# Every fifth piece of the mixer's weights: its low part on GpSimd instead of VectorE

## The chip, the core and the metric

One core of one Trainium2 chip runs the whole program. The metric is device time in microseconds for one execution; each version is run several times and the median counts.

## What is computed

A decoder trunk of two layers over 256 tokens of width 1024, in float32. Cut to what matters here:

```python
for layer in range(2):
    y   = h @ w_in[layer]                  # 256x1024 @ 1024x3672: q, k, v, gates, indexer of three mixers
    mix = concat(gla(y), moba(y), dsa(y)) @ w_out[layer]      # w_out 1024x1024
    h   = layer_norm(alpha * h + mix)
    h   = layer_norm(alpha * h + moe(h))   # router, 16 experts of width 512, top 2
```

`w_in` and `w_out` are the mixer's weights; the experts' weights are not touched by the change.

## The kernel before

**Stages.** The profiled span shows two layers. The mixer of layer 0 runs from 0 to about 146 us, its experts to about 355, the mixer of layer 1 from 355 to about 501, its experts to the end. Weights stream in over SyncE's queue into 33 feed buffers (`wf`) and are used once.

**The split product.** In the mixer, a matrix product in float32 is made of three products in the faster type fp32r. Activations and weights are each split into a high part (rounded to fp32r) and a low part (what the rounding lost), and TensorE adds high x high, high x low and low x high in one PSUM bank. In the trace the weights' parts are `whi` and `wlo`, the activations' `hhi` and `hlo`. ScalarE makes `whi` by a copy with rounding; VectorE makes `wlo` by subtracting `whi` from the weights `wf`, so that this subtraction has two inputs in SBUF.

**Pieces.** The class `Pieces` (line 573) does this for the weights. `weight_pieces(l)` writes the plan of a layer in the order in which TensorE wants it: groups I (16 pieces of 292 columns), V (8 of 512), GV (16 of 264), M, S, GK, GG (8 of 512 each) from `w_in`, then 16 of 512 from `w_out`; 88 in all, counted from 0 by `self.i`. Before TensorE takes piece j, `fill` makes the pieces up to j + `ahead` (4 in most of the mixer, 5 in the first group, 3 for `w_out`). When all pieces of a feed buffer are made, `more()` issues the next weight DMA. In layer 1 the first two pieces are made ahead of the layer norm by `fill(pool)` (line 1648), so their low parts are GpSimd's already. The first group of each layer multiplies the first 128 tokens in plain float32 with unsplit weights, then the other 128 with the pieces.

**What else is on the engines.** VectorE has, among other things, the indexer's sums (`acc`, a chain of eight dependent operations for each score block, then loops of max and replace), the rotary embedding (`rope`, on `yk` and `yq`), softmax steps, and the split of the activations of layer 1 (`hlo`). GpSimd has the powers of the norms, a memset for the linear attention (`aM`), and in layer 1 two operations on the 128x1024 tile `z`, a multiply and an add (`pool.tensor_mul(z, z, g2)`, `pool.tensor_add(z, z, b2)`), both called a z multiply below for short.

**The order.** The schedule is written by hand (`manual_schedule`): each engine runs its list strictly in the order in which the program emits it. The class `Order` keeps an estimated clock for each engine; generators wait ("yield") until something they need is due by these clocks, and so the estimates decide which operation is emitted next. `_Lane.cost` has the estimates: 1.04 n + 65 ns for a subtraction of n columns on VectorE, 2.2 n + 50 on GpSimd (lines 205 to 215). All operations go through one helper, so that the profile puts nearly all on its line 235; operations are told apart by their tiles.

Of the kernel before, what the change touches and what calls it, by code (L numbers as in the profile page):

```python
# [9 lines left out]
F32 = mybir.dt.float32  # L10
# [34 lines left out]
N_T4 = 9  # L45
N_SM = 10
N_WS = 4
N_WO = 3
N_UNITS = ((1, 3), (2, 6))
N_WARM0 = 7  # L50
# [189 lines left out]
def trunk_kernel(ctx, tc, x, positions, w_in, gate_up, gate_bias, norm_gain, w_out, ln_mix_g, ln_mix_b,  # L240
# [8 lines left out]
    pe, act, dve, pool = od.pe, od.act, od.dve, od.pool  # L249
# [9 lines left out]
    def t2(name, shape=(P, 512), dt=F32):  # L259
        return wp.tile(list(shape), dt, name=name, tag="t2", bufs=N_T2)  # L260
# [80 lines left out]
    def more(n=1):  # L341
        for _ in range(n):
            while issued[0] < len(specs) and specs[issued[0]][0] in extra:
                issued[0] += 1
            if issued[0] >= len(specs):
                return
            key, (parts, nk, w) = specs[issued[0]]
            issued[0] += 1
            t = fp.tile([P, nk, w], F32, name="wf", tag="wf")
            for at, src in parts:  # L350
                nc.sync.dma_start(t[:, at[0], at[1]] if at else t.rearrange("p k n -> p (k n)"), src)
            feed[key] = t
# [220 lines left out]
    class Pieces:  # L573
# [8 lines left out]
        def fill(self, eng=dve):  # L582
            while self.i < len(self.plan) and self.i < self.j + self.ahead:
                key, kk, c0, n = self.plan[self.i]
                src = feed[key][:, kk, c0:c0 + n]
                hi = t2("whi", (P, n), F32R)
                lo = t2("wlo", (P, n), F32R)
                act.activation(hi, src, AF.Copy)
                eng.tensor_sub(lo, src, hi.bitcast(F32))
                units[key] = feed[key]  # L590
                self.made[self.i] = hi, lo
                self.left[key] -= 1
                if not self.left[key]:
                    feed.pop(key)
                    more()
                self.i += 1
# [72 lines left out]
    def weight_pieces(l):  # L669
# [5 lines left out]
        for k0 in OUT_ORDER:  # L675
            plan += [((l, "O", k0 + kk), 0, 512 * n, 512) for kk in range(2) for n in range(2)]
        return Pieces(plan, N_WS)

# [83 lines left out]
    for l in range(DEPTH):  # L762
        done = set()

        def project(widths, res, first, step):
# [3 lines left out]
            if first:  # L769
                pieces.ahead = N_AHEAD  # L770
                for k in range(KT):
# [9 lines left out]
                    yield None  # L781
                pieces.ahead = N_WS
            for k in range(KT):
# [339 lines left out]
        def backbone():  # L1123
# [28 lines left out]
            n_done = 0  # L1152
            pieces.ahead = N_WO
            for k0 in OUT_ORDER:
# [559 lines left out]
```

## Time and profile before

| | |
|---|---|
| median of 3 runs | 723.16 us (722.4 to 724.0) |
| the profiled execution | 724.48 us |
| its span, first to last instruction | 722.8 us |
| TensorE busy | 696.5 us (96%) |
| VectorE busy | 440.6 us (61%) |
| ScalarE busy | 267.9 us (37%) |
| GpSimd busy | 43.9 us (6%) |
| granted TensorE clock, mean | 0.989 |
| DMA | 244.05 MB, 338 GB/s |

Engines are called PE (TensorE), PEld (its weight load), DVE (VectorE), ACT (ScalarE), POOL (GpSimd). A row of the order of time gives the start in us, the length, engine, line, operation, the tiles (out<-in), the shape, how many were merged into the row, and in brackets the engine's idle time just before, with what ended it. Busy shares are averages over stages that differ; the mixers are 292 us of the span.

### The profile page before, as it was taken

To read this page: it belongs to the slowest core of one execution; us is meant where nothing else is said; L and a number is where in the kernel's file an instruction comes from. 1 tells how busy PE (TensorE), PEld (TensorE's weight loads), DVE (VectorE), ACT (ScalarE), POOL (GpSimd) and SP (SyncE) were. 2 spreads that over 40 slices of the span, in tenths; PEclk is the share of its full clock that TensorE was granted. 3 is DMA by queue.
4 is the path that set the end of the run, shared out by engine and by line. 5 is a ranking of instruction groups with operands and counts; after the bars stand their busy time and mean duration, and the time that the engine had idled before them with its cause. 6 is when DMAs were issued, how large, how long until landed. Compare 5 with 4: busy or idle time off the path is not lost. (4 is left out here: it accounts for less than half of the span.)

```text
span 722.8 us, 11139 instructions
## 1 busy us (share of the span) xinstructions
PE 696.5 (96%) x3829; PEld 405.7 (56%) x3829; DVE 440.6 (61%) x1115; ACT 267.9 (37%) x547; POOL 43.9 (6%) x72
## 2 busy tenths in 40 slices
PE   9999999999999989999899999999999999999993
PEld 8897977853533533533488889777535334343330
DVE  6787865650635455767488688757243546358645
ACT  5667655431312112212186666464213112022121
POOL 2000001000000001210130000011000000011002
PEclk9999999999999999999999999999999999999997
DMA  9799945869999999999999754469699999999971
GB/s 308 274 388 408 409 162 204 298 225 408 408 404 408 406 406 409 407 409 408 333 391 400 306 184 163 152 227 338 236 409 409 403 407 408 406 409 409 408 301 58
DMA packets 83533, 244.05 MB, mean 338 GB/s; under 512 B 10180, under 2 KB 14344, under 8 KB 83464
## 3 DMA queue, kind: packets, MB, share of 16 engines
q1 hardware_dynamic: 82792, 242.91, 88.1%
q8 instruction: 34, 0.56, 0.3%
q10 hardware_dynamic: 416, 0.26, 0.1%
q14 instruction: 35, 0.29, 0.1%
q0 software_dynamic: 256, 0.03, 0.0%
HBM read 242.13 MB, written 1.05 MB: 336 GB/s over the span
## 5 line engine op out<-in xcount | busy, mean ns | idle before, releaser
L235 PE MATMUL gu<-wf,xT 128*64 128x512 f32 x912 | 226.0, 594 | 3.5 <-PEq L1430 3.5
L235 PEld LDWEIGHTS gu<-wf,xT 128*64 128x64 f32 x912 | 71.8, 137 | 131.7 <-issue 123.6
L235 DVE SCALAR_TENSOR_TENSOR yt<-y,ws,yt 32x512 fp32r<-32x512 f32 (+1 forms) x116 | 86.7, 748 | 94.6 <-ACT yt L235 93.2
L235 DVE TENSOR_TENSOR wlo<-wf,whi 128x512 fp32r<-128x512 f32 (+2 forms) x174 | 97.2, 598 | 44.5 <-ACT whi L235 40.3
L235 PE MATMUL y<-wf,actT 128*64 128x512 f32 x432 | 110.5, 595 | 1.8 <-ACT actT L235 1.8
L235 ACT ACTIVATE whi<-wf 128x512 fp32r<-128x512 f32 (+2 forms) x176 | 86.8, 551 | 16.5 <-PE po L235 9.5
L235 PE MATMUL pj<-whi,hhi 128*128 128x512 f32 (+2 forms) x224 | 81.7, 365 | 0.0
L235 PE MATMUL pj<-wlo,hhi 128*128 128x512 f32 (+2 forms) x224 | 78.1, 349 | 1.7 <-DVE wlo L235 1.5
L235 PE MATMUL pj<-whi,hlo 128*128 128x512 f32 (+2 forms) x224 | 77.7, 347 | 0.0
L235 ACT ACTIVATE yt<-y,ws 128x512 fp32r<-128x512 f32 x60 | 36.9, 687 | 104.2 <-PE y L235 91.1
L235 PEld LDWEIGHTS y<-wf,actT 128*64 128x64 f32 x432 | 34.2, 137 | 53.8 <-issue 40.5
L235 DVE TENSOR_TENSOR act<-act,gu 128x512 f32<-128x512 f32 x16 | 11.0, 688 | 83.9 <-PE gu L235 64.9
L235 PE MATMUL gu<-wx,xT 128*64 128x512 f32 x112 | 52.7, 596 | 0.0
L235 PEld LDWEIGHTS pj<-whi,hhi 128*128 128x128 f32 x224 | 42.1, 188 | 8.2 <-issue 2.9
L235 PEld LDWEIGHTS pj<-wlo,hhi 128*128 128x128 f32 x224 | 42.1, 188 | 7.2 <-DVE wlo L235 3.5
L235 PEld LDWEIGHTS pj<-whi,hlo 128*128 128x128 f32 x224 | 42.0, 188 | 5.2
L235 ACT ACTIVATE actT<-aT 128x512 f32<-128x512 f32 x16 | 9.5, 595 | 85.3 <-PE aT L235 76.7
L235 ACT ACTIVATE xT<-xT,cols 128x256 f32<-128x256 f32 x32 | 17.4, 564 | 60.1 <-PE xT L235 60.1
L235 ACT ACTIVATE act<-gu 128x512 f32<-128x512 f32 x16 | 9.6, 597 | 76.2 <-PE gu L235 76.2
L235 PE MATMUL y<-wx,actT 128*64 128x512 f32 x80 | 33.4, 595 | 0.0
L235 DVE TENSOR_TENSOR z<-z,sc 128x512 f32<-128x512 f32 x48 | 29.7, 680 | 0.4 <-PE sc L235 0.4
L235 DVE TENSOR_SCALAR xT<-xT,cols 128x256 f32<-128x256 f32 x32 | 16.9, 543 | 14.7 <-ACT xT L235 14.3
(269 smaller groups left out, 938.0 us busy)
## 6 DMA issues: line engine op xcount, KB each, us to landing
wf<-in_w_expert_gate_dram SPq DMA_DIRECT2D x114, 512.0 KB, 10.2
wf<-in_w_expert_up_dram SPq DMA_DIRECT2D x114, 512.0 KB, 9.9
wf<-in_w_expert_down_dram SPq DMA_DIRECT2D x108, 512.0 KB, 10.1
wf<-in_w_in_dram SPq DMA_DIRECT2D x32, 512.0 KB, 9.9
wx<-in_w_expert_down_dram SPq DMA_DIRECT2D x36, 256.0 KB, 6.0
wf<-in_w_out_dram SPq DMA_DIRECT2D x16, 512.0 KB, 11.0
wx<-in_w_expert_up_dram SPq DMA_DIRECT2D x24, 256.0 KB, 6.7
wx<-in_w_expert_gate_dram SPq DMA_DIRECT2D x10, 512.0 KB, 7.4
```

The source lines that it names most:

```text
L235: return fn(*a, **kw)
```

## The change

A constant and one expression. In `Pieces.fill`, the subtraction of the pieces with index 4, 9, 14, ... goes to GpSimd's list (`pool`), the others stay with `eng`, which is VectorE except in the call `fill(pool)`. The planner then books the subtraction on GpSimd's clock with GpSimd's estimate.

```diff
+SHARE = 5
@@ class Pieces, fill
                 act.activation(hi, src, AF.Copy)
-                eng.tensor_sub(lo, src, hi.bitcast(F32))
+                (pool if self.i % SHARE == SHARE - 1 else eng).tensor_sub(lo, src, hi.bitcast(F32))
```

## Rows read from the trace of the kernel before

**Rows 1.** Busy time by stretch (engine busy and count, PEclk, DMA share, GB/s).

```profile
0.00:146.00 146.00, 144.18 (x901) 120.00 (x905) 107.11 (x319) 87.97 (x194) 9.43 (x33) 1.00 0.85 307
...
355.00:501.00 146.00, 143.19 (x899) 117.38 (x900) 112.62 (x304) 88.60 (x196) 13.43 (x12) 1.00 0.75 269
```

**Rows 2.** TensorE's waits, 0 to 146 us: total, times, longest.

```profile
PE pj L235 <- DVE wlo L235: 0.7, 1, 0.7
```

**Rows 3.** TensorE's waits, 355 to 501 us.

```profile
PE pj L235 <- DVE wlo L235: 0.8, 2, 0.6
```

**Rows 4.** Groups by form: count, busy us, mean ns, idle before.

```profile
L235 DVE TENSOR_TENSOR wlo<-wf,whi 128x512 fp32r<-128x512 f32 x112 | 73.5, 686 | 36.0 <-ACT whi L235 33.7 <-PE po L235 2.0
...
L235 POOL TENSOR_TENSOR wlo<-wf,whi 128x292 fp32r<-128x292 f32 x2 | 1.6, 806 | 46.3 <-ACT whi L235 46.3
```

**Rows 5.** Order of time: GpSimd's work on z and VectorE beside it.

```profile
365.19 2.51 POOL L235 TENSOR_TENSOR z<-z,vec 128x1024 f32<-128x1024 f32 x1 [3.08 <-PE tr L235]
...
367.00 1.25 DVE L235 TENSOR_TENSOR hlo<-hT,hhi 128x512 fp32r<-128x512 f32 x1 [0.24 <-ACT hhi L235]
...
367.77 2.70 POOL L235 TENSOR_TENSOR z<-z,vec 128x1024 f32<-128x1024 f32 x1
...
368.17 2.86 DVE L235 TENSOR_TENSOR hlo<-hT,hhi 128x512 fp32r<-128x512 f32 x1
...
358.23 0.75 DVE L235 SCALAR_TENSOR_TENSOR z<-z,mv,vec 128x512 f32<-128x512 f32 x1
...
714.65 1.26 POOL L235 TENSOR_TENSOR z<-z,vec 128x512 f32<-128x512 f32 x1 [0.34 <-ACT z L235]
...
714.94 1.53 DVE L235 SCALAR_TENSOR_TENSOR z<-z,mv,vec 128x512 f32<-128x512 f32 x1
```

**Rows 6.** Layer 0 near 60 us: order of time; groups up to 62.2 us.

```profile
57.48 1.29 DVE L235 TENSOR_TENSOR wlo<-wf,whi 128x512 fp32r<-128x512 f32 x2 [3.45 <-ACT whi L235]
...
58.90 0.62 ACT L235 ACTIVATE whi<-wf 128x512 fp32r<-128x512 f32 x1
...
59.66 2.68 DVE L235 SCALAR_TENSOR_TENSOR acc<-rl,wi,acc 128x128 f32<-128x128 f32 x7
62.26 1.89 DVE L235 TENSOR_TENSOR wlo<-wf,whi 128x512 fp32r<-128x512 f32 x3
...
63.00 0.50 PE L235 MATMUL pj<-wlo,hhi 128*128 128x512 f32 x1 [0.73 <-DVE wlo L235]
...
L235 DVE TENSOR_TENSOR wlo<-wf,whi 128x292 fp32r<-128x292 f32 (+2 forms) x47 | 22.0, 519 | 12.9 <-ACT whi L235 12.9
```

**Rows 7.** The same place in layer 1, order of time.

```profile
415.07 0.62 ACT L235 ACTIVATE whi<-wf 128x512 fp32r<-128x512 f32 x1
...
416.06 0.34 DVE L235 SCALAR_TENSOR_TENSOR acc<-rl,wi,mc 128x128 f32<-128x128 f32 x1
...
419.03 0.68 DVE L235 TENSOR_TENSOR wlo<-wf,whi 128x512 fp32r<-128x512 f32 x1
...
419.77 0.50 PE L235 MATMUL pj<-wlo,hhi 128*128 128x512 f32 x1
```

**Rows 8.** The start of layer 1: pieces 4, 9 and those after.

```profile
364.47 0.44 ACT L235 ACTIVATE whi<-wf 128x292 fp32r<-128x292 f32 x1
...
369.78 0.43 ACT L235 ACTIVATE whi<-wf 128x292 fp32r<-128x292 f32 x1
...
372.16 4.18 DVE L235 TENSOR_TENSOR wlo<-wf,whi 128x292 fp32r<-128x292 f32 x11
...
372.66 0.40 PE L235 MATMUL pj<-wlo,hhi 128*128 128x292 f32 x1 [0.57 <-DVE wlo L235]
```

**Rows 9.** Layer 1, piece 19 and the rope chain.

```profile
377.48 0.62 ACT L235 ACTIVATE whi<-wf 128x512 fp32r<-128x512 f32 x1
...
378.48 0.16 DVE L235 TENSOR_TENSOR rope<-yk,rc 128x16 f32<-128x16 f32 x1
...
381.64 0.33 PE L235 MATMUL tr<-ident,yk 128*128 128x128 f32 x1 [0.20 <-DVE yk L235]
```

## The prediction

> **What bounds the kernel now.** I read the table of busy time by stretch first, since the change touches only the two mixers (0 to 146 and 355 to 501 us). In it the reader is to see that TensorE is busy 144.18 of 146 us in the first mixer and 143.19 of 146 in the second, VectorE 107.11 and 112.62, ScalarE 88, GpSimd 9.43 and 13.43, with the granted clock at 1.00, which is the 2.4 GHz level [rows 1]. So TensorE sets the pace, VectorE is three quarters full, and GpSimd is nearly free. The second view is what TensorE waited for in each mixer. In the first only one wait on a low part (wlo) stands, 0.7 us; in the second two, 0.8 us together [rows 2, 3]. All that a lighter VectorE could give back directly is therefore about 1.5 us of some 289. The third view is the order of time around these waits and around GpSimd's work: a kernel whose TensorE is this full gains or loses only where a wlo comes just in time or too late.
>
> **What is moved.** Each layer's plan has 88 pieces (16 of 292 columns, 16 of 264, 56 of 512). Of the indices 0 to 87, those with remainder 4 by five are 4, 9, ... 84: 17 a layer, 34 in all (3 of 292, 4 of 264, 10 of 512 in each layer). The high part stays on ScalarE, no DMA moves, and no piece changes its place on TensorE's list by itself.
>
> **Taken from VectorE.** A 512-column subtraction lasts 0.686 us [rows 4]; back to back they start (1.89 - 0.68) / 2 = 0.60 us apart [rows 6]. 34 pieces at no more than that are under 20.4 us of the 219.7 us that VectorE is busy in both mixers. Off TensorE's path this is worth nothing.
>
> **Added to GpSimd.** It has made two 292-column low parts already: 0.806 us each [rows 4]. For 512 columns the nearest row is its z multiply of 128x512, 1.26 us [rows 5]. Per layer 3 x 0.81 + 4 x about 0.75 + 10 x 1.26 = 18 us (0.75 is an estimate for 264 columns from the two rows), on an engine idle for over 130 of 146. A moved piece is thus about 0.6 us slower than VectorE would be alone, but pieces are made three to five ahead, and a moved one no longer queues behind VectorE's other work. I cost the longer latency at nothing; the cover is the other pieces that TensorE multiplies meanwhile, and if it were gone, a piece would cost up to 0.6 us.
>
> **What the two engines do to each other** is the term that decides. In layer 1 GpSimd multiplies z at 365.19 (2.51 us) and again at 367.77 (2.70 us, to 370.48). VectorE's subtractions hlo <- hT - hhi have the form of wlo (two SBUF inputs, fp32r out, 512 columns). The first, 367.00, takes 1.25 us and ends 0.55 after GpSimd's first; the second, 368.17, takes 2.86 us and ends 371.03, again 0.55 after GpSimd's second [rows 5]. Alone such an operation takes 0.69 [rows 4]. So VectorE stands still until GpSimd is through. The second z multiply in turn waited for the first hlo (to 368.25) and then needed 2.23 us, where the undisturbed one took 2.51: about 0.28 us of GpSimd's time is a start that needs no memory port. The three-operand form does the same: z <- z,mv,vec takes 1.53 us at 714.94 beside GpSimd and 0.75 at 358.23 without it [rows 5]. The price of one moved piece to a busy VectorE is hence 1.26 - 0.28 = 0.98 us for 512 columns (0.81 - 0.28 = 0.53 for 292), against 0.60 (0.37) given back later, where the piece's own turn would have been: VectorE gets slower, not faster, while it has two-input work queued. The bounds of one meeting are 0 (it finds VectorE idle or with a PSUM operand) and 0.98.
>
> The Trainium skill (SBUF — State Buffer, section Who interferes with whom) says that a VectorE instruction with two SBUF inputs and a GpSimd instruction that reads SBUF exclude each other, the second one blocking fully. By that rule the trace agrees (2.86 us), and were the port merely shared, a meeting would cost about half and the sum below 1.7 us. The skill (Perfetto Trace Analysis, section Optimizing Scalar/DVE Operations) allows offloading to GpSimd if VectorE is saturated, and warns that it might not help between these two; here VectorE is not saturated (107 of 146 us).
>
> **Where it lands on TensorE's path.** Pieces are counted by wlo in VectorE's list: 47 of them (0 to 46) start before 62.2 [rows 6].
> 1. Layer 0, piece 49. Its high part ends at 58.90 + 0.62 = 59.52 [rows 6]. GpSimd starts near 59.58 and wants the port at 59.86, inside the chain of eight acc operations (two SBUF inputs each; the last seven from 59.66, 2.68 us). It gets it at the next joint, 60.02, and holds it to 61.0, so the third operation (60.05) is 0.95 late. Behind the chain stand the wlo of pieces 47, 48 and 49 at 62.26; TensorE already waits for 47 (63.00, idle 0.73) [rows 6]. So +0.95. That piece 49 is no longer third there helps nobody: TensorE is at 47.
> 2. Layer 1, piece 49, the same place. High part done at 415.07 + 0.62 = 415.69; GpSimd wants the port at 416.03 and gets it when VectorE's subtraction before the chain ends, about 416.1; it holds it to 417.1, so the first acc operation of the chain, 416.06, ends at about 417.4 in place of 416.40. Piece 48's wlo at 419.03 ends at 419.72, and TensorE takes it at 419.77 [rows 7]. No slack: +1.0.
> 3. Layer 1, piece 4. High part done at 364.91 [rows 8]. GpSimd works from 364.97 to 365.78, and its z multiply, behind it in its queue, starts at about 365.76 instead of 365.19. Both multiplies and the hlo that they block move by 0.57, then the run of eleven wlo from 372.16 (pieces 5 to 15), on whose first TensorE waits at 372.66, idle 0.57 [rows 5, 8]. +0.57.
> 4. Layer 1, piece 9. High part done at 370.21 [rows 8], so it runs right after the z multiplies and takes the port between the second hlo and the third: +0.53 for the same run of wlo. From there the run, eleven in 4.18 us, is a little faster than TensorE uses it and has two members fewer (9 and 14), so I cost piece 14's meeting at nothing.
> 5. Layer 1, piece 19. High part done at 378.11; GpSimd wants the port at about 378.45, and the rope chain starting at 378.48 waits 0.95. The piece's own 0.60 is given back where its turn was, between the chain's two halves, so its end comes 0.35 later; TensorE turns yk at 381.64, waiting 0.20 for VectorE already [rows 9]. +0.35.
> The other 29: TensorE waits for no wlo near them [rows 2, 3], and what a meeting takes is mostly given back when the piece's own turn falls out (net 0.98 - 0.60 = 0.4 us for 512 columns, some 0.1 for 264). I cost them at nothing; the end of the bound is 3 us, if the eight 264-column ones and a few others use up the room that there is.
>
> Sum: 0.95 + 1.0 + 0.57 + 0.53 + 0.35 = 3.4 us. TensorE cannot get it back, since it is 98% busy otherwise, and the experts that follow start later by as much. The profiled execution took 724.48 us (its span 722.8 and 1.7 around it), 1.3 above the median of the runs, 723.16; it would become 727.9, and the median 723.16 + 3.4 = 726.6.
>
> **The order.** Order, the planner, costs a GpSimd subtraction at 2.2 n + 50 = 1176 ns for 512 columns and VectorE's at 597, and writes every engine's list by these clocks. With VectorE freer in its book some operations (the selection loops above all, which are let out by VectorE's clock) will be listed earlier. I can't read the new lists from this trace; it can shift each of the five places by a position, up or down. This is most of my range.
>
> **The rivals.**
> A. VectorE's relief reaches TensorE: faster. The mechanism is that a late wlo comes sooner since a moved subtraction was queued ahead of it. The price is the waits for wlo, 0.7 + 0.8, and 0.2 for yk: 721.5. Against it: ahead of the late pieces 47 (layer 0) and 48 (layer 1) stands the acc chain, not a moved piece, and earlier VectorE was idle 3.45 us waiting for ScalarE, at 57.48 [rows 6], so what piece 44 frees is lost there. It decides only if the new lists take the chain out from ahead of those pieces. 0.09.
> B. The meetings fall where VectorE is idle or in loops with one input, or the lists move piece 49 off the chain: 0 to 1.4 us, 723 to 724.6. 0.21.
> C. GpSimd is late itself: a moved piece queued behind a pow, a memset that waits for its buffer, or the z multiplies, with TensorE waiting for it, or the small rooms of the 264-column run used up: 2 to 4 us on top, 728.5 to 731. For it: GpSimd's list is in order. Against it: in the lists as they are, only piece 9 stands behind long work. 0.12.
> The forecast, 724.6 to 728.5, has 0.58. That the pieces stay on VectorE can't be: one expression picks the engine.
>
> **How the numbers follow.** Predicted 726.6. The range leaves out A's half and C's upper part: 722.4 to 729.8. A measurement of this kernel can tell about 0.2% (1.45 us) from no change. Slower than 724.6: the forecast and C, 0.70; within: B, 0.21; faster than 721.7: A, 0.09.
>
> **What would show it.** In the new profile: 36 wlo on GpSimd, 512-column ones near 1.26 us or longer where they wait; single acc, rope and hlo operations of VectorE stretched by about 1 us next to them; TensorE's wait for wlo grown from 1.5 to 4 or 5 us; VectorE's busy time falling by clearly less than 20 us. I am wrong if the seven acc operations still take 2.68 us beside a GpSimd piece, if TensorE waits for a GpSimd wlo, or if TensorE's instructions stand in another order and the idle moves with them.

## The result, and the profile after

Five runs of each on one chip: 734.11 us with the change (730.61 to 736.41) against 723.96 before (722.4 to 724.19), a ratio of 1.0149, 95% interval 1.0128 to 1.0170. That is 10.1 us slower. The forecast was 726.6 with 722.4 to 729.8 as its range: the sign was right, the size a third of what came.

The profiled execution of the changed kernel took 730.61 us, its span 728.9. First the page's busy time by engine, changed kernel:

```profile
PE 695.9 (95%) x3829; PEld 402.4 (55%) x3829; DVE 442.6 (61%) x1081; ACT 268.9 (37%) x547; POOL 81.4 (11%) x106
```

VectorE executes 34 instructions fewer (1115 before) and is busy 2.0 us longer than the 440.6 of before. GpSimd gained 37.5 us (43.9 before), where 2 x 18 were forecast. The table of busy time by stretch says the same of the first mixer, where VectorE had 107.11 [rows 1]; the columns are as there:

```profile
0.00:146.00 146.00, 142.56 (x871) 117.73 (x872) 106.67 (x297) 86.82 (x190) 27.19 (x49) 1.00 0.83 299
```

The stretch has 22 VectorE operations fewer, of which 17 are the moved subtractions and the rest come only after 146 us by now, and VectorE is as busy as it was. In the page's costliest groups the low parts stand as 140 and 36 [rows 4 have 112 of 512 columns and 2]:

```profile
L236 DVE TENSOR_TENSOR wlo<-wf,whi 128x512 fp32r<-128x512 f32 (+2 forms) x140 | 85.9, 643 | 41.5 <-ACT whi L236 38.3
...
L236 POOL TENSOR_TENSOR wlo<-wf,whi 128x512 fp32r<-128x512 f32 (+2 forms) x36 | 40.5, 1125 | 235.2 <-ACT whi L236 204.3
```

Where TensorE's time went: its waits in the first mixer (0 to 147 us), then in the second (355 to 511); total, times, longest. Before there were 0.7 and 0.8 us for wlo [rows 2, 3] and 0.2 for `yk` [rows 9]; rows left out belong to the start, the norm and the router, or are of 0.5 us and less.

```profile
PE pj L236 <- DVE wlo L236: 1.7, 1, 1.7
PE tr L236 <- DVE y L236: 0.5, 1, 0.5
...
PE pj L236 <- DVE wlo L236: 1.9, 2, 1.6
...
PE rw L236 <- DVE mc L236: 1.1, 1, 1.1
PE tr L236 <- DVE y L236: 1.0, 2, 0.7
PE tr L236 <- DVE yk L236: 0.9, 1, 0.9
...
PE tr L236 <- DVE og L236: 0.5, 1, 0.5
```

The waits for wlo are 3.6 us in place of 1.5. What is new in kind is the rest: TensorE now also waits for VectorE's results of the mask (`mc`), the rotary embedding (`y`, `yk`) and the output gate (`og`). None waits for GpSimd.

How long each mixer takes is read in TensorE's order of time, from the first product of the split pieces to the first logit of the router (start, length):

```profile
14.30 0.51 PE L236 MATMUL pj<-whi,hhi 128*128 128x292 f32 x1
...
146.76 0.65 PE L236 MATMUL lgT<-zT,mc 128*32 128x128 f32 x16
...
370.16 0.51 PE L236 MATMUL pj<-whi,hhi 128*128 128x292 f32 x1
...
507.38 0.65 PE L236 MATMUL lgT<-zT,mc 128*32 128x128 f32 x16
```

132.46 and 137.22 us. The same four rows before stand at 14.61, 144.52, 369.58 and 499.98: 129.91 and 130.40. So the mixers lost 2.55 and 6.82, together 9.4 us, against 10.1 by the medians. This measure is worked out the same way for every run below, from one profiled execution of each kernel. It is steadier than the time: in e7 and e9 below, which change nothing ahead of the second mixer, the first comes within 0.1 us of before. And here is why the time is not. The table by stretch, before and then after, for the five microseconds behind each mixer:

```profile
150.00:155.00 5.00, 5.00 (x29) 4.94 (x30) 1.59 (x11) 0.66 (x2) 0.00 (x0) 0.66 0.46 184
505.00:510.00 5.00, 4.54 (x27) 4.51 (x28) 1.99 (x13) 0.80 (x2) 0.00 (x0) 0.66 0.57 224
```

```profile
150.00:155.00 5.00, 3.90 (x32) 3.58 (x32) 3.70 (x28) 1.66 (x3) 0.00 (x0) 1.00 1.03 390
505.00:510.00 5.00, 4.61 (x53) 3.48 (x52) 4.38 (x15) 2.89 (x7) 1.87 (x3) 1.00 1.03 399
```

The granted clock (third number from the end) is 0.66 before and 1.00 after: in the profiled execution of before, 3.4 us of each stretch ran at the lower level, 1.2 GHz, which costs about 1.7 us a time, and in that of after neither did. (The stretches hold different work, since after is later by then.) So the profiled spans differ by only 6.1 us: 9.4 less 2 x 1.7 is 6.0. Executions of one kernel differ in this; by mean granted clock, before took about 721.0 at 0.994 and 724.7 at 0.989, and after 730.6 at 0.994 and about 734 at 0.989: 9.6 and about 9.3 us apart at equal clock, close to the 9.4 of the mixers.

Three of the places show what a meeting does; these are orders of time of the changed kernel. The forecast's first place, layer 0, piece 49:

```profile
59.69 1.27 POOL L236 TENSOR_TENSOR wlo<-wf,whi 128x512 fp32r<-128x512 f32 x1 [7.96 <-ACT whi L236]
...
59.76 1.35 DVE L236 SCALAR_TENSOR_TENSOR acc<-rl,wi,acc 128x128 f32<-128x128 f32 x1
...
64.08 0.50 PE L236 MATMUL pj<-wlo,hhi 128*128 128x512 f32 x1 [1.73 <-DVE wlo L236]
```

One acc operation lasts 1.35 where seven took 2.68 [rows 6], and TensorE idles 1.73 instead of 0.73: the forecast was 0.95, measured 1.0. A place that the forecast did not have, in layer 1, piece 44:

```profile
409.87 3.24 DVE L236 SCALAR_TENSOR_TENSOR acc<-rl,wi,acc 128x128 f32<-128x128 f32 x6
...
410.92 1.27 POOL L236 TENSOR_TENSOR wlo<-wf,whi 128x512 fp32r<-128x512 f32 x1 [9.96 <-ACT whi L236]
...
413.37 0.38 PE L236 MATMUL rw<-mc,ones 128*128 128x128 f32 x1 [1.06 <-DVE mc L236]
```

Six acc in 3.24, where 6 x 0.383 = 2.30 is usual (2.68 / 7 from [rows 6]); the mask behind them comes 0.94 late, and TensorE waits 1.06 for it. And a third, piece 59 beside the rotary embedding; the first row is the same operation undisturbed, 0.99 us earlier:

```profile
438.92 0.29 DVE L236 TENSOR_TENSOR rope<-y,rs 128x128 f32<-128x128 f32 x1
...
439.76 1.38 POOL L236 TENSOR_TENSOR wlo<-wf,whi 128x512 fp32r<-128x512 f32 x1 [8.88 <-ACT whi L236]
439.91 1.38 DVE L236 TENSOR_TENSOR rope<-y,rs 128x128 f32<-128x128 f32 x1
...
441.83 0.41 PE L236 MATMUL tr<-ident,y 128*128 128x128 f32 x2 [0.74 <-DVE y L236]
```

0.29 becomes 1.38, and TensorE waits 0.74. Neither of these two kinds of place cost anything in the kernel before; the views of [rows 2, 3] had no `mc` and no `y`. Two things are mixed in the result, then: GpSimd's piece holds VectorE up, and both engines' lists are written in another order, so that the pieces meet other work. The experiments take them apart.

### The profile page after: what moved, and what is told of

Same layout as the page of the kernel before. It is cut to its first block, busy times and chain, and to the rows that moved or that the text cites. A ratio compares the mean times of both kernels' runs of the same rounds, so it can differ in the third digit from the quotient of the medians.

```text
span 728.9 us, 11172 instructions
## 1 busy us (share of the span) xinstructions
PE 695.9 (95%) x3829; PEld 402.4 (55%) x3829; DVE 442.6 (61%) x1081; ACT 268.9 (37%) x547; POOL 81.4 (11%) x106
## 3 DMA queue, kind: packets, MB, share of 16 engines
HBM read 242.13 MB, written 1.05 MB: 334 GB/s over the span
## 5 line engine op out<-in xcount | busy, mean ns | idle before, releaser
L236 DVE TENSOR_TENSOR wlo<-wf,whi 128x512 fp32r<-128x512 f32 (+2 forms) x140 | 85.9, 643 | 41.5 <-ACT whi L236 38.3
L236 POOL TENSOR_TENSOR wlo<-wf,whi 128x512 fp32r<-128x512 f32 (+2 forms) x36 | 40.5, 1125 | 235.2 <-ACT whi L236 204.3
L385 POOL DMA_DIRECT2D vec<-in_ln_mix_g_dram x2 | 1.5, 771 | 256.2 <-PE y L236 128.1
## 6 DMA issues: line engine op xcount, KB each, us to landing
wf<-in_w_expert_gate_dram SPq DMA_DIRECT2D x114, 512.0 KB, 10.1
wf<-in_w_expert_up_dram SPq DMA_DIRECT2D x114, 512.0 KB, 10.1
```

Source lines behind the costliest of these rows:

```text
L236: return fn(*a, **kw)
L385: nc.gpsimd.dma_start(t[0:1], dram(arr, l * D, [D, 1], [1, D]))
```

## Experiments

In each the `fill` line is the one changed, unless said. Ratios are against runs of the kernel before on the same chip, with 95% intervals; "mixers" is the measure above, as a difference from before.

**e1: the new lists, the work left on VectorE.** The planner books every fifth piece on GpSimd, but VectorE executes it.

```diff
+    booked_pool = _Lane(od, nc.vector, "POOL")
-                eng.tensor_sub(lo, src, hi.bitcast(F32))
+                (booked_pool if self.i % 5 == 4 else eng).tensor_sub(lo, src, hi.bitcast(F32))
```

> The lists of the change without its engine: the planner books the 34 subtractions on GpSimd's clock at GpSimd's estimate, as in the change, but VectorE does them. If the loss comes from the two engines shutting each other out of SBUF (theory P, port), this stands near the kernel before, 723 to 725.5 us. If it comes from the lists that the planner rewrites (theory L, lists), it stands near the kernel after, 730 to 735. If TensorE waits for pieces that GpSimd makes late (theory G), 723 to 725.5 too.

Measured: 1.0049 [1.0032, 1.0065], mixers +0.94 and +3.02. TensorE's waits in the second mixer:

```profile
PE pj L235 <- DVE wlo L235: 0.8, 2, 0.6
...
PE tr L235 <- DVE yk L235: 0.9, 1, 0.9
```

The waits for wlo are those of before; the one for `yk` is the changed kernel's, as is one of 0.6 for `y` in the first mixer. Lists written for a VectorE that does less, on a VectorE that does all, cost 4.0 us by themselves, without a moved piece to meet. The time, 726.04, lies between the two expectations: neither theory alone gives the loss. TensorE's instructions stand in this trace in the order of the changed kernel, one by one, so that the two can be laid side by side.

**e2: the new engine, the old lists.** GpSimd executes the pieces, the planner books them as VectorE's.

```diff
+    booked_dve = _Lane(od, nc.gpsimd, "DVE")
+                (booked_dve if self.i % 5 == 4 else eng).tensor_sub(lo, src, hi.bitcast(F32))
```

> The engine of the change without its lists: GpSimd does the 34 subtractions, but the planner books them on VectorE's clock at VectorE's estimate, so that every other operation stands where it stood before. Theory P: 726.6 (my five places) to 734, with VectorE's operations stretched beside GpSimd's. Theory L: 723 to 726. Theory G: 727 to 734, with TensorE's waits naming GpSimd's wlo.

Measured: 726.72, 1.0049 [1.0025, 1.0073], mixers +1.04 and +2.78, together 3.8. Order of time at place 1, then TensorE's waits in the first and the second mixer:

```profile
59.77 1.27 POOL L235 TENSOR_TENSOR wlo<-wf,whi 128x512 fp32r<-128x512 f32 x1 [7.97 <-ACT whi L235]
59.83 3.67 DVE L235 SCALAR_TENSOR_TENSOR acc<-rl,wi,acc 128x128 f32<-128x128 f32 x7
```

```profile
PE pj L235 <- DVE wlo L235: 1.7, 1, 1.7
...
PE pj L235 <- DVE wlo L235: 3.0, 3, 1.6
PE tr L235 <- DVE yk L235: 0.5, 1, 0.5
```

Seven acc operations last 3.67 in place of 2.68: 0.99, where the price of a meeting was worked out as 0.98. This kernel is the one that the forecast described (726.6), since its lists are those that could be read from the trace before; but it is not the changed kernel. Lists alone (4.0) and engine alone (3.8) add up to 7.8 of the 9.4 us; the other 1.6 come only where both are there.

**e3: GpSimd only writes, old lists.** As e2, but GpSimd sets the low part to zero, twice, so that it is occupied without reading; the low part of these 34 pieces is left out of the product.

```diff
+                eng.tensor_sub(lo, src, hi.bitcast(F32)) if self.i % 5 != 4 else (
+                    od.note('DVE', dve.cost('tensor_sub', lo, [src, hi], {}), [src, hi], [lo]),
+                    [nc.gpsimd.memset(lo.bitcast(F32), 0.0) for _ in range(2)])
```

> As the engine without the lists, but GpSimd fills the 34 low parts with zeros, twice each, in place of subtracting: it writes about as long and reads nothing (left out: the low part of these pieces). Theory P, with the read port as what is shared: no stretched two-input operations on VectorE, and since VectorE has 34 subtractions less, 722 to 724. Were it the time of GpSimd's writes or its place in the list, the loss of the run with subtractions would stay, 727 to 734.

Measured: 0.9998 [0.9978, 1.0018], mixers -0.02 and -0.62. The page's busy time by engine, then TensorE's waits in the second mixer:

```profile
PE 693.9 (96%) x3829; PEld 402.5 (56%) x3829; DVE 423.7 (59%) x1081; ACT 267.9 (37%) x547; POOL 73.4 (10%) x140
...
PE pj L235 <- DVE wlo L235: 0.6, 2, 0.4
```

Here VectorE is relieved as the change means it to be: 423.7 us, 16.9 less than before, with GpSimd almost as busy (73.4 to 81.4) and the same 1081 instructions on VectorE as in e2 and the change. So GpSimd's being occupied and its writes cost TensorE nothing here; the 3.8 us of e2 hang on what it reads. (Zeros need no high part and land earlier than the subtraction would, but in e2 TensorE waits for nothing from GpSimd, so the landing is not the cause either.) The Trainium skill (SBUF — State Buffer, section Who interferes with whom) has a VectorE instruction with two SBUF inputs contend with a GpSimd instruction that reads SBUF and not with one that only writes; this pair of runs agrees, 3.8 us with reads and -0.6 without. It also bounds the relief: with 34 subtractions simply gone and nobody in the way, the kernel gains 0.6 us in the mixers, and by its time nothing that can be told from zero.

**e4: piece 49 alone.** The two largest places, nothing else; lists as before.

```diff
+                (booked_dve if self.i == 49 else eng).tensor_sub(lo, src, hi.bitcast(F32))
```

> Only piece 49 of each layer on GpSimd, everything else and all lists as before. Theory P by the forecast's terms: 0.95 + 1.0 = 1.95 us, so 725 to 726.5; the acc operation that meets GpSimd's piece is stretched by about 1 us and TensorE's wait for piece 47 (layer 0) and 48 (layer 1) grows by it. Theories L and G: 723 to 724.

Measured: 723.28, 1.0007 [0.9991, 1.0022]; mixers +1.04 and +0.96. The time alone would have denied the 1.95 us that the forecast gave these two; the mixers show 2.0. All but one of its runs had a granted clock of 0.993 or 0.994, at which before took about 721.0, so the half-speed stretches that fell away hid the loss: 723.2 against 721.0 at that clock. I take the mixers as the reading, and the time as inconclusive.

**e5: the changed lists, VectorE really freed.** Booked as the change books them; GpSimd sets zeros twice as in e3 (low part of 34 pieces left out).

```diff
+                    od.note('POOL', pool.cost('tensor_sub', lo, [src, hi], {}), [src, hi], [lo]),
```

> The lists of the change with the 34 low parts filled with zeros by GpSimd, twice each, in place of the subtraction (left out: the low part of these pieces). VectorE is then as free as the planner booked it, and GpSimd reads nothing. If the new lists are bad in themselves (theory L), the loss of the run with the lists alone stays: 726 to 727. If they are good lists for a VectorE that is freer than the real one, and what breaks them is that VectorE is held up beside GpSimd (or, in the run with the lists alone, still has the 34 subtractions), this stands near the kernel before: 721.5 to 724.

Measured: 0.9990 [0.9974, 1.0006], mixers +0.33 and +1.14. TensorE's waits in the second mixer hold none for `yk`, `y`, `mc` or `og` of 0.2 us or more:

```profile
PE pj L235 <- DVE wlo L235: 0.6, 2, 0.4
PE tr L235 <- ACT whi L235: 0.3, 1, 0.3
```

VectorE's busy time is 424.8 here. The same lists that cost 9.4 us in the changed kernel cost 1.5 where VectorE has the time that the planner booked. (At 0.993 and above, 722.4 against 721.0, the 1.4 us show in the time too.)

**e6: e2 without the five forecast places**, to see whether the other 29 cost nothing.

```diff
+                (booked_dve if self.i % 5 == 4 and (key[0], self.i) not in ((0, 49), (1, 4), (1, 9), (1, 19), (1, 49)) else eng).tensor_sub(...)
```

> The engine without the lists, but the five places of the forecast stay on VectorE (layer 0: piece 49; layer 1: pieces 4, 9, 19, 49); the other 29 are GpSimd's. By the forecast's terms these cost nothing: 722 to 723.7, TensorE's waits for wlo as before (0.7 and 0.8 us). If they use up the room (the forecast's upper bound): up to 725.7.

Measured: 1.0038 [1.0020, 1.0055], mixers +0.06 and +3.70. A miss: 3.8 us where nothing was expected, and a wait of a kind that neither e2 nor the changed kernel has:

```profile
PE pj L235 <- POOL wlo L235: 2.0, 1, 2.0
```

It is for piece 14 of layer 1. Behind that wait the granted clock fell as well: in the 7 us from 376 it is 0.76, with a stretch at 1.2 GHz beginning at 378.6. So 2.0 us and some 1.7 make the 3.7. Of the other 28 one can be seen: behind piece 59 TensorE waits 0.3 us longer for `y`, as in e2.

**e9: piece 14 of layer 1 alone**, lists as before.

```diff
+                (booked_dve if (key[0], self.i) == (1, 14) else eng).tensor_sub(lo, src, hi.bitcast(F32))
```

> Only piece 14 of layer 1 on GpSimd, all lists as before. In the run with the 29 pieces this one began at 373.7 us beside VectorE's back-to-back run of subtractions and lasted 4.57 us, to the end of that run, with TensorE idle for 2.1 us behind it; in the run with all 34 and the old lists it began beside the same run and lasted 0.92. If GpSimd, once it has missed its turn, stays shut out for as long as VectorE's two-input operations follow each other without a gap, the piece alone shows it again and costs 2 us of waiting, and more if the granted clock falls after it: 724.5 to 727. If the long piece was an accident of that one execution: 722.5 to 723.5.

Measured: 726.05, 1.0047 [1.0030, 1.0065], mixers 0 and +1.78. One piece of 34 costs in the time about as much as all 34 in e2, in the mixers half of that (at a clock of 0.989, where most of its runs were, 726.0 against 724.7 before; the rest of its 3.3 us is the clock). Six of its seven runs had a clock of 0.989 or less, and five of the 23 of before, so the piece may bring the lower clock itself; that was not tried further. Order of time:

```profile
370.15 5.62 DVE L235 TENSOR_TENSOR wlo<-wf,whi 128x292 fp32r<-128x292 f32 x13
...
371.86 4.57 POOL L235 TENSOR_TENSOR wlo<-wf,whi 128x292 fp32r<-128x292 f32 x1 [3.38 <-PE pj L235]
...
376.48 0.40 PE L235 MATMUL pj<-wlo,hhi 128*128 128x292 f32 x1 [1.95 <-POOL wlo L235]
```

Here VectorE does not wait: thirteen subtractions run back to back, ten of 292 columns and three of 512, each as long as undisturbed, and GpSimd's, 0.81 alone [rows 4], lasts 4.57, to 376.43, 0.66 after VectorE's run ends at 375.77. In e2 the same piece begins inside such a run too, and takes 0.92 (order of time, e2):

```profile
374.52 0.92 POOL L235 TENSOR_TENSOR wlo<-wf,whi 128x292 fp32r<-128x292 f32 x1 [2.78 <-ACT whi L235]
...
374.68 1.07 DVE L235 TENSOR_TENSOR wlo<-wf,whi 128x292 fp32r<-128x292 f32 x1
```

It took the port at the next joint, and VectorE's next subtraction took 1.07. In the changed kernel the same piece lasts 0.91. Why it is let in there and shut out in e9 and e6 stays open.

**e10: the change, with a planner that is told that VectorE gains nothing.** The piece is booked on both clocks.

```diff
+                (pool if self.i % 5 == 4 else eng).tensor_sub(lo, src, hi.bitcast(F32)); od.clk['DVE'] += (1.04 * n + 65) * (self.i % 5 == 4)
```

> The change, but the planner's book is told that VectorE gains nothing: each moved piece is booked on GpSimd as in the change, and VectorE's clock is also moved on by what the subtraction would have cost there. Its lists then reckon with a VectorE as busy as it really is. If the part of the loss beyond the forecast's comes from lists written for a freer VectorE, it goes: like the run with the old lists, 725.5 to 728. If not, the loss stays at 730 to 735.

Measured: 726.59, 1.0052 [1.0034, 1.0070], mixers +1.35 and +2.46, together 3.8. TensorE's waits in the first and the second mixer:

```profile
PE pj L235 <- DVE wlo L235: 1.7, 1, 1.7
...
PE pj L235 <- DVE wlo L235: 2.9, 3, 1.6
PE tr L235 <- DVE yk L235: 0.5, 1, 0.5
```

The waits for `mc`, `y` and `og` are gone, and what is left has the size of e2's loss and its waits (0.3 us more in the first mixer, 0.3 less in the second). GpSimd does the same 34 subtractions as in the changed kernel; only the planner's book differs. It takes back 5.6 of the 9.4 us in the mixers, by the medians 6.3 of 10.1 (10.1 less 726.59 - 722.75 = 3.8). Its lists are close to those of before and not the same: some operations still stand elsewhere, far fewer than in the changed kernel.

**e7, e8, e11: what could be kept.** Since [rows 5] show GpSimd's z multiplies in VectorE's way before the change, e7 moves no piece and emits the z operations later. e8 adds two pieces that stand in front of a waiting TensorE, 47 in layer 0 and 48 in layer 1, on GpSimd with the old lists. e11 has these two pieces alone.

```diff
e7, e8:
-                yield lambda: f"hT{nxt}{t}1" in od.ready
+                yield lambda: "v" in gl
e8, e11:
+                (booked_dve if (key[0], self.i) in ((0, 47), (1, 48)) else eng).tensor_sub(lo, src, hi.bitcast(F32))
```

> No piece is moved; only the two GpSimd operations on z of layer 1 are listed later, after the GV group, where VectorE has idle time. Theory P: the subtractions hlo of layer 1 are no longer stretched (0.69 us each in place of 1.25 and 2.86), TensorE's wait at the first group of layer 1 (0.57 us) goes, and the time falls by 0.6 to 0.8 us: 721.8 to 722.3. If the waits came from elsewhere: no change in TensorE's wait there.

> z later as in the run before this, and two pieces on GpSimd, chosen as those that TensorE waited for because they stood behind the acc chain on VectorE: 47 in layer 0 and 48 in layer 1, booked as before. Theory P: they are ready before TensorE asks, the chain is held up by about 0.5 us, which costs nothing; the waits of 0.73 and about 0.25 us go as well. Sum 0.89 + 0.25 + 0.73 = 1.9 us: 720.5 to 721.5. If GpSimd's help cannot reach TensorE at all: as the run before this.

> Two pieces on GpSimd, lists as before: 47 in layer 0 and 48 in layer 1, which TensorE waited for because they stood behind the acc chain on VectorE; the operations on z stay in their place. TensorE's waits of 0.73 us and about 0.25 us go, the chain is held up by half a microsecond each: 721.5 to 722.5 beside 722.6, at the edge of what timing can tell; the order of time shows it. If moving a piece can only cost: 723 or more.

Measured: e7 1.0004 [0.9982, 1.0027], mixers 0 and +0.15; e8 0.9990 [0.9973, 1.0008], -0.48 and +0.14; e11 0.9997 [0.9981, 1.0013], -0.49 and -0.05. Two of the three missed their range: e7 took 723.06 (721.8 to 722.3 expected) and e8 722.20 (720.5 to 721.5). In e7 the wait at 372.66 [rows 8] is gone, but GpSimd now runs z beside two low parts that stand just ahead of the second mixer's first acc chain, and two low parts behind that chain's start come late (TensorE's order of time, e7):

```profile
391.39 0.39 PE L235 MATMUL pj<-wlo,hhi 128*128 128x264 f32 x1 [0.24 <-DVE wlo L235]
...
393.79 0.39 PE L235 MATMUL pj<-wlo,hhi 128*128 128x264 f32 x1 [0.57 <-DVE wlo L235]
```

The meeting was moved, not removed. The two pieces of e11 take away the wait at 63.00 [rows 6], 0.5 us in the mixer, and its time can't be told from before. No version here is shown to beat the kernel before.

## Why the prediction came out so

**Right: what bounds it, and that relief is worth nothing.** TensorE was the bound; with the subtractions gone and no contention (e3) the mixers gain 0.6 us and the time nothing clear of noise. VectorE's busy time was to fall by clearly less than 20 us; it rose by 2.0. Adding up in the order of time what VectorE's operations beside a GpSimd piece took above the usual of their form, over what before had of that, gives 9.5 us in the first mixer (13 operations) and 8.4 in the second, 17.9 in all, where e3 puts the relief at 16.9.

**Right: the price of a meeting and the five places, on the lists that they were read from.** In e2, in the order of the sum, by the time from one TensorE instruction to the next, against before (both kernels have the same TensorE list):

| place | forecast | e2 |
|---|---|---|
| 1. layer 0, piece 49 | 0.95 | 1.00 |
| 2. layer 1, piece 49 | 1.0 | 1.01 |
| 3, 4. layer 1, pieces 4 and 9 | 1.10 | 1.05 |
| 5. layer 1, piece 19 | 0.35 | 0.27 |
| mixers | 3.4 | 3.8 |

Of what the five leave, 0.28 is the wait for `y` behind piece 59.

**Wrong: the step "The order".** It says that the new lists "can shift each of the five places by a position, up or down". I took the new lists for a disturbance without a sign, and gave it the range's two sides. Here they had one. With the change the planner books 17 subtractions a layer fewer on VectorE, 3 x 0.369 + 4 x 0.340 + 10 x 0.597 = 8.4 us by its own estimate (1.04 n + 65), and it writes the lists of all engines for that VectorE. I had already worked out that VectorE would get nothing, and did not carry that into the planner. TensorE's list then asks for a result of VectorE before it is there: in layer 1 the two transposes of `yk` stand behind 18 products of group V before and in e2, and behind 15, one piece earlier, in e1 and the changed kernel. e1 shows the cost without a moved piece (+4.0 us), e5 shows that the same lists are nearly harmless where VectorE is really freed (+1.5), e10 that booking the truth takes back 5.6 us of 9.4.

In the changed kernel the five places were not merely shifted by a position. Against before, by the time between TensorE's instructions: place 1 +1.0; places 3 and 4 +1.05; place 5 +0.95 instead of 0.35; place 2 is gone, and a wait of 0.25 with it. In the order of time piece 19 (place 5) reads, in the changed kernel, then VectorE's row in e2, then TensorE's in e1:

```profile
379.91 1.30 POOL L236 TENSOR_TENSOR wlo<-wf,whi 128x512 fp32r<-128x512 f32 x1 [3.50 <-ACT whi L236]
...
379.99 1.25 DVE L236 TENSOR_TENSOR rope<-yk,rc 128x16 f32<-128x16 f32 x1
...
383.63 0.33 PE L236 MATMUL tr<-ident,yk 128*128 128x128 f32 x1 [0.88 <-DVE yk L236]
```

```profile
379.02 1.25 DVE L235 TENSOR_TENSOR rope<-yk,rc 128x16 f32<-128x16 f32 x1
...
381.98 0.33 PE L235 MATMUL tr<-ident,yk 128*128 128x128 f32 x1 [0.88 <-DVE yk L235]
```

A rope operation of 0.16 [rows 9] takes 1.25. It does so in e2 too, where TensorE's wait grew by 0.27 only; in e1, with none of the moved pieces on GpSimd, it grew by 0.67 (0.88 idle, as in the changed kernel). Together these are the 0.95: the meeting cost what was forecast, and the order came on top. The new waits for `mc` (1.18 beyond the usual distance of two products), `y` (0.71 in layer 0; 0.71 and 1.35 in layer 1), `og` (0.71), and three smaller (0.40, 0.32, 0.49) add 5.87. The sum is 1.0 + 1.05 + 0.95 + 5.87 - 0.25 = 8.6 of the 9.4 us. e1, with the same TensorE list, tells which of them need a meeting. The wait for `y` in layer 0 (0.73 in e1), the 0.71 for `y` in layer 1 (0.6 in e1) and the 0.49 are there in e1 as well: they are the order, without a meeting. Those for `mc`, for `og`, the later one for `y` and the 0.40 and 0.32 are not, so they need the pieces on GpSimd; and they need the new lists, since e2 and e10 have none for `mc` and `og`, and for `y` 0.28 at most.

**Wrong: "The other 29" at nothing.** Nearly true of 28 in e6 (0.3 us). Piece 14 costs 1.8 to 2.0 us where it is shut out (e6, e9). I had its meeting with the long run of wlo as VectorE's delay, and never as GpSimd's. In the changed kernel it did no harm, so this is a mistake that did not move the result.

**The rivals.** A's mechanism can be seen in e11, on the two pieces that it needs, at 0.5 us in a mixer; the change does not move these. B's condition, an idle VectorE or a loop with one input, held for about a third of the pieces of e2: beside the others a VectorE operation is stretched, `s_sb<-s_sb,ri` with one tensor input among them (see the end). Most of these meetings cost TensorE nothing all the same. C, a TensorE that waits for GpSimd, was priced at 2 to 4 us and is what e6 and e9 have; the changed kernel, which landed beyond its 731, has no such wait. So the range was too narrow above for a cause of its own: "The order" had a position at each of five places as its bound, where the planner books 8.4 us a layer away from VectorE. What share of that TensorE would feel could not be read from the trace before; e1 and the pair e2 and after put it at 4.0 to 5.6 us in both mixers together.

**What would show it.** 36 wlo on GpSimd, stretched acc, rope and hlo operations, VectorE hardly relieved: seen. A wait for wlo of 4 to 5 us: 3.6. "TensorE's instructions stand in another order and the idle moves with them" was named as what would make me wrong, and it is what came, through what the planner booked for VectorE.

## What to carry to other kernels

Where a planner writes the lists, a wrong cost of an operation is a change to all lists: if a moved operation frees its old engine less than the planner books (here by nothing, for the shared port), cost the lists by the engine as it will be, and try the move with the old lists first (e2 against the change: 3.8 against 9.4 us). Moved two-input operations took about as much out of VectorE here as they had taken before (17.9 for 16.9 us), at places that the mover did not choose. And where the clock falls to half for a few microseconds in some executions, compare stretches of the trace as well as times: e4 would have been read wrongly by its time.

## What the runs showed of the hardware that was not expected

- The port between the two engines is not always won by the one that waits: GpSimd's 292-column subtraction lasted 4.57 us in e9 (and 4.57 in e6) beside back-to-back subtractions on VectorE, and 0.92, 0.91 and 0.91 in e2, the changed kernel and e10. Each began within a VectorE operation; what decides is open.
- Not only operations with two tensor inputs are held up. `s_sb<-s_sb,ri`, a TENSOR_SCALAR of 0.34 us, took 1.19 beside a GpSimd subtraction in e2 (at 88.77), and 2.08 in the changed kernel (at 102.31) beside a subtraction and the memset of `aM` right behind it. A memset only writes, and still in the kernel before `acc<-acc`, a TENSOR_SCALAR of 0.23 at 91.16, took 0.93 at 448.36 beside that of `aM`.
- Short stretches at the 1.2 GHz level, behind the mixers, appear in some executions and not in others of one kernel, and cost about 1.7 us each. In e6 one stood inside the second mixer instead, after TensorE had idled 2.0 us; in the profiled execution of e9, with an idle of 1.95 at the same place, none did. What makes them come was not tried.
